# The first FFN's opening stage: fewer, larger contraction groups, and every partial product added by VectorE out of PSUM

## The chip, the cores and the metric

The kernel runs on one core of one Trainium2 chip. The metric is the device time of one execution in microseconds (us). All times below are read from the runs of this kernel or from its profile, which was taken on the chip.

The engines are called by short names: PE (TensorE, the matmuls; PEld is its weight load), DVE (VectorE), ACT (ScalarE), POOL (GpSimd) and SP (SyncE, which here only issues DMAs). SBUF is the on-chip working memory, PSUM the memory into which PE accumulates.

## The reference

One layer of a hybrid encoder on 256 tokens of width 2048, in float32. The part that matters here is the first feed-forward network (FFN) and the modulation in front of it:

```python
mod = (silu(c) @ w_ada + b_ada).reshape(B, 9, D)         # D = 2048
sh1, sc1, ga1, ... = mod
h = rms_norm(x, g_ffn1) * (1.0 + sc1) + sh1
x = x + 0.5 * ga1 * ((silu(h @ w1_a) * (h @ w3_a)) @ w2_a)   # D_FF = 5632
```

Then follow the mixer (latent attention and gated linear attention, merged by gates), a second FFN of the same form, and a last norm. `w_ada` is 2048 x 18432; `w1_a` and `w3_a` are 2048 x 5632.

## The kernel before

**Products.** Every float32 product is computed from exact parts. A weight tile `raw` is split into `wh` (ACT, line 97) and `wl = raw - wh` (DVE, line 98); the activations are kept transposed as `hTh` and `hTl`, 128 rows of the contraction per tile. `mm3` (lines 108 to 111) then issues three matmuls, `wh*hTh`, `wl*hTh` and `wh*hTl`, for each of the two token blocks of 128 tokens.

**Weights.** All weights pass through one ring of three 1 MB buffers, `raws` (line 46), filled by DMAs that SP issues in order. The parts go to `wh` and `wl`, six buffers of 1024 columns each (line 47): one `raw` gives two of each. A unit of `w_ada` goes through the same ring: `ada_unit` (line 159) loads 1 MB and multiplies it by the row `c_bc` on DVE with a running sum (line 163), which gives one column of 128 entries of `mod`.

**The opening stage.** The normed and modulated `h` needs, for each 128 rows of the contraction (`kt`, 16 of them), two columns of `mod` (shift and scale), so two `w_ada` units. The kernel does not wait for all 32. It walks the contraction in groups (`GROUPS`, line 397): as soon as the columns of a group are there, it makes the `h` rows of that group and multiplies them with the matching rows of `w1_a` and `w3_a` for the first six chunks of 512 columns (`NPRO`, line 396). That makes 12 partial products per group (6 chunks, two matrices), each 256 x 512. A partial product goes into a PSUM tile `pacc` (two such tiles, line 49) and is then added to a running sum in SBUF, `sums` (line 494). The loop at lines 458 to 513 emits this raw tile by raw tile; four 128 x 512 weight tiles share one raw buffer, so there are 48 of them.

**How a partial product is added (lines 493 to 508).** The first group's go to `sums` by an ACT copy. Of the later ones, one in three (`ADD_DVE`, line 398) is added by DVE straight from PSUM (line 503). The others are copied by ACT to `ev` (line 507) and added by POOL in SBUF (line 508). In the last group the product of `w1_a` is copied by ACT (line 500) and added by POOL (line 501), then goes through silu on ACT (line 510); that of `w3_a` is added by DVE; POOL multiplies the two (line 512).

**The rows of h.** `xn_T` (line 287) scales the rows of `x` and transposes them on PE; `mod_T` (line 296), here with `early=True`, applies scale and shift on ACT (line 306), casts `hTh` on ACT (line 311) and subtracts to `hTl` on POOL (line 312).

**What sets the order.** `AHEAD` (line 401) says how many raw tiles ahead of a group's first raw tile all of its `w_ada` units must have been issued; between these marks `target` (line 449) spreads the units evenly. `LEAD` and `XLEAD` say how early `mod_T` and `xn_T` are emitted. The program order so written is not yet the order of each engine's queue: a scheduler takes the instructions by program order as their operands become ready by its own estimate, and fixes one order for each engine. On the chip each engine then runs its list in that order.

After the stage come `ffn_down` for the six chunks (line 517), and the remaining five chunks with the plain loop `ffn_up`.

Of the kernel before, what the change touches and what calls it, by code (L numbers as in the profile page):

```python
# [31 lines left out]

# offsets of the columns of `cols`
C_BADA, C_GF1, C_GMX, C_GF2, C_GQL, C_GKV, C_GQN, C_GKN = 0, 144, 160, 176, 192, 196, 200, 201
# offsets of the parts of `rows`
R_GQR, R_GKR, R_GGLA, R_FREQ = 0, 64, 128, 384
# [3 lines left out]
def layer_kernel(ctx: ExitStack, tc: tile.TileContext, a: dict):  # L40
# [17 lines left out]
    def wkA(name):  # L58
        return wk.tile([P, 1024], F32, tag="wA", name=name)
# [3 lines left out]

    # ------------------------------------------------------------ constants
    x_sb = const.tile([P, TB, D], F32, name="x_sb")
# [14 lines left out]

    # ------------------------------------------------------------ weights
    def load_unit(ap, width=2048):
# [4 lines left out]
    def split_raw(raw, src_cols, n):  # L87
        """exact parts of raw[:, :src_cols], as pairs of n columns"""
        res = []
        per = max(1, (src_cols // n) // 2)  # L90
        k = 0
        while k * n < src_cols:
            w = min(per * n, src_cols - k * n)
            wh = hl.tile([P, 1024], F32R, tag="wh", name="wh")
            wl = hl.tile([P, 1024], F32R, tag="wl", name="wl")
            src = raw[:, k * n:k * n + w]
            ACT.copy(wh[:, :w], src)  # L97
            DVE.tensor_tensor(wl[:, :w], src, wh[:, :w].bitcast(F32), op=ALU.subtract)  # L98
            for q in range(w // n):
                res.append((wh[:, q * n:(q + 1) * n], wl[:, q * n:(q + 1) * n]))  # L100
            k += w // n
        return res

    def unit_parts(ap, nkt, n):
        """one weight unit: nkt tiles of n columns"""
        return split_raw(load_unit(ap, nkt * n), nkt * n, n)
# [8 lines left out]
    def gemm(acc, units, n=512, tbm=None, mid=None, hook=None):  # L115
        """acc[tok, n] = x^T W over the units (ap, nkt, k0, xs); units tbm[0]:tbm[1] are
        done for one token block and then for the other"""
        total = sum(u[1] for u in units)
# [35 lines left out]

    # ------------------------------------------------------------ adaLN columns
    ada_q = []
# [14 lines left out]
    def need(j, kt):  # L171
        """issue what is queued up to the unit that gives column kt of mod j"""
        while (j, kt) not in ada_done:
            fill(1)
# [7 lines left out]
    def load_c(pool, first=False):  # L182
        """silu(c) on every partition"""
        c_bc = pool.tile([P, D], F32, tag="cbc", name="c_bc")
        if not first:
            ACT.dma_start(c_bc, a["c"].to_broadcast([P, D]))
            ACT.activation(c_bc, c_bc, AF.Silu)
            return c_bc
        SP.dma_start(c_bc[0:1, :], a["c"])
        ACT.activation(mod[:, 0:16], mhalf, AF.Silu)  # L190
        ps = bank("warm")
        for _ in range(WARM):
            PE.matmul(ps[:, 0:P], ones, ones, start=True, stop=True)
        ACT.activation(c_bc[0:1, :], c_bc[0:1, :], AF.Silu)
        for kg in range(4):
            ps = bank("c_ps")
            PE.matmul(ps, ones[0:1, :], c_bc[0:1, kg * 512:(kg + 1) * 512], start=True, stop=True)
            ACT.copy(c_bc[:, kg * 512:(kg + 1) * 512], ps)
        return c_bc

    def mod_cols(i, lo, hi, c_g):
        """columns lo:hi of (a, b) of norm i"""
        sh, sc = 3 * i * 16, (3 * i + 1) * 16
# [11 lines left out]
    def gate_rows(pool, i, scale, name):  # L215
        """gate i as rows broadcast over the partitions, 512 columns at a time"""
        j = 3 * i + 2
# [23 lines left out]

    # ------------------------------------------------------------ norm into T layout
    ss_t = const.tile([P, TB, 4], F32, name="ss_t")
# [23 lines left out]
    def next_hT(i):  # L267
        """a list that takes h^T of norm i, and what fills it for a token block"""
        hT = []
# [13 lines left out]
    def norm_T(hT, i, tb, k0, nk):  # L283
        """rows k0*128.. of h^T of norm i, in exact parts"""
        mod_T(hT, i, tb, k0, nk, xn_T(tb, k0, nk))
# [10 lines left out]
    def mod_T(hT, i, tb, k0, nk, ps, early=False):  # L296
# [14 lines left out]
        ACT.copy(hi, hv)  # L311
        (POOL if early else DVE).tensor_tensor(lo, hv, hi.bitcast(F32), op=ALU.subtract)  # L312

    # ------------------------------------------------------------ FFN
    def ffn_act(acc1, acc3):
        """silu(acc1) * acc3"""
        s = wkA("silu")
# [6 lines left out]
    def ffn_gT(g, ring, name):  # L324
        """g transposed, in exact parts: [P, 2, 4, S]"""
        gT = ring.tile([P, 2, 4, S], F32R, tag="ring", name=name)
# [12 lines left out]
    def resid(acc, g, n, tbs, tail=False, then=None):  # L339
        """x += acc * gate for the 512 columns n of the token blocks tbs"""  # L340
        nt = len(tbs)
# [12 lines left out]
    def add_product(units, g, n, tail, then, tbm, hook=None):  # L354
        """x += gate * (product) for the 512 columns n"""
        g(n)
# [37 lines left out]

    # ================================================================ FFN 1
    NPRO = 6
    GROUPS = (1, 1) + (2,) * 7
    ADD_DVE = 3
    LEAD = 3
    XLEAD = 1  # L400
    AHEAD = lambda gi: (0, 1, 0, 1, 2, 3, 4, 5, 5)[gi]
    ADA_END = 5
    RATE = 0.75
    LATE = 1
    with tc.tile_pool(name="f1", bufs=1, reuse_waits="tile") as f1, \
# [36 lines left out]
        n_all = len(ada_q)  # L442
        # ada units that have to be issued before a raw tile
        marks = [(0, 2 * GROUPS[0])]
# [13 lines left out]
        for r, grp in enumerate(raws_of):  # L458
# [23 lines left out]
            for gi, c, wi, k in grp:  # L482
# [12 lines left out]
                if gi == 0:  # L495
                    ACT.copy(sums[c][:, wi], acc)
                elif gi == len(GROUPS) - 1 and wi == 0:
                    pre = wkA("silu")
                    pv = pre.rearrange("p (t n) -> p t n", t=TB)
                    ACT.copy(pv, acc)  # L500
                    POOL.tensor_tensor(pv, pv, sums[c][:, 0], op=ALU.add)
                elif (c * 2 + wi) % ADD_DVE == 0 or gi == len(GROUPS) - 1:
                    DVE.tensor_tensor(sums[c][:, wi], acc, sums[c][:, wi], op=ALU.add)  # L503
                else:
                    ev = wkB("ev")
                    evv = ev.rearrange("p (t n) -> p t n", t=TB)
                    ACT.copy(evv, acc)  # L507
                    POOL.tensor_tensor(sums[c][:, wi], sums[c][:, wi], evv, op=ALU.add)  # L508
                if gi == len(GROUPS) - 1 and wi == 1:
                    ACT.activation(pre, pre, AF.Silu)  # L510
                    g = wkB("gact")
                    POOL.tensor_tensor(g, sums[c][:, 1].rearrange("p t n -> p (t n)"), pre, op=ALU.mult)
                    late.append(g)

# [10 lines left out]

    # ================================================================ mixer
    xs = xs_of(hT)
# [15 lines left out]
    with tc.tile_pool(name="mx", bufs=1, reuse_waits="tile") as mx:  # L543
# [4 lines left out]
        with tc.tile_pool(name="mla", bufs=1, reuse_waits="tile") as ml:  # L548
            # ---- rotary tables
            posi = ml.tile([P, TB], I32, name="posi")  # L550
# [66 lines left out]

            # ---- latents
            def latent(parts, c_g, name):
                """RMS-normed latent, transposed, in exact parts; parts: per token block 512 columns"""  # L620
                junk = wkA("junk")
# [36 lines left out]
            kv_done, ckv = latent([acc[:, tb] for tb in range(TB)], C_GKV, "ckv")  # L658
            # query latent, k_rope and g_lr: columns [q 0:256 | k_rope], [q 256:512 | g_lr]
            accs = [acc_tile("qc0"), acc_tile("qc1")]  # L660
# [11 lines left out]

            # ---- k_rope | g_lr
            def rope(dst, src, tab, nh):
                """dst, src [P, TB, nh, 64]"""
                ta, tbb = tab
# [38 lines left out]
            def mla_pair(hp, k_hook):  # L715
                """latents up for two heads; returns the stages of their attention"""
                v4 = lambda t, d: t.rearrange("p (t h d) -> p t h d", t=TB, h=2)
# [135 lines left out]
        with tc.tile_pool(name="late", bufs=1, reuse_waits="tile") as lt, ExitStack() as ctx2:  # L853
# [5 lines left out]
            with tc.tile_pool(name="gla", bufs=1, reuse_waits="tile") as gl:  # L859
# [38 lines left out]
                def gla_head(h, hook):  # L898
                    """one head; returns the stages behind its projections"""
                    hs = slice(h * P, (h + 1) * P)  # L900
# [145 lines left out]

    # ================================================================ FFN 2
    with tc.tile_pool(name="f2", bufs=1, reuse_waits="tile") as f2, \
# [36 lines left out]
def _units(w):  # L1085
    """[K, N] -> [K/512, N/512, 128, 4*512]: 512x512 blocks, rows k*128+p at partition p"""
    K, N = w.shape
# [58 lines left out]
```

## Time and profile before

| | |
|---|---|
| time, median of 3 runs | 2260.61 us (2259.78 to 2260.78) |
| span of the profiled execution, first to last instruction | 2255.0 us |
| time of the median run beyond that span | 5.6 us |
| mean granted TensorE clock | 0.981 |
| first and last start of a matmul into `pacc` | 19.0 and 402.6 us |
| busy in the first 405 us: PE, DVE, ACT, POOL | 326.5, 365.4, 212.2, 233.7 us |

No time of its own is listed for the profiled execution beside its span; the 5.6 us are the difference between the median of the runs and that span. Busy times are sums of the profile's records of an engine; matmuls are pipelined, so a busy PE is not a PE at its peak. Line numbers are those of the kernel before. A row of a group reads: line, engine, operation, output and inputs with their shapes, count, then busy microseconds, the mean nanoseconds of one, and the engine's idle time just before them with what ended it.

### The profile page before, as it was taken

The numbers are of one execution on the slowest core, as the hardware profiler recorded it, in microseconds if no ns is written. First come the engines' busy times: TensorE is split into PE (matmuls) and PEld (weight loads), VectorE is DVE, ScalarE is ACT, GpSimd is POOL, SyncE is SP. The second block draws the span as 40 slices with busy tenths as digits, with TensorE's granted clock in tenths as the row PEclk, the third lists the DMA queues.
The fourth block names the chain that finished last, engine by engine and source line by source line (L and its number), as shares of the span: only waits on it lengthen the run. The fifth ranks groups of instructions, "written<-read, shape, count | busy, mean of one in ns | idle before, by whom it ended". The sixth has DMA issues, their size and how long they took to land.

```text
span 2255.0 us, 24933 instructions
## 1 busy us (share of the span) xinstructions
PE 2161.3 (96%) x9652; PEld 1763.1 (78%) x9652; DVE 1578.9 (70%) x1604; ACT 1044.3 (46%) x1279; POOL 276.6 (12%) x148
## 2 busy tenths in 40 slices
PE   8788788999999999999999999999999999999998
PEld 5566566788888887988777788878888888888886
DVE  6999898888787787756566667766666455444454
ACT  6545455433433445555564444455444433444443
POOL 1766557100000000001000000000000000000000
PEclk8899899999999999999999999999999999999999
DMA  8667675799898884644576777866777555555553
GB/s 297 230 233 253 227 248 192 276 352 347 334 336 324 328 318 148 227 145 165 195 256 245 257 262 278 296 235 241 281 287 268 191 208 196 189 193 187 194 189 112
DMA packets 87305, 549.16 MB, mean 244 GB/s; under 512 B 10322, under 2 KB 10626, under 8 KB 28435
## 3 DMA queue, kind: packets, MB, share of 16 engines
q1 hardware_dynamic: 84242, 539.97, 66.4%
q0 software_dynamic: 1344, 3.17, 0.5%
q10 hardware_dynamic: 1602, 4.44, 0.5%
q8 instruction: 75, 1.23, 0.2%
q14 instruction: 42, 0.34, 0.0%
HBM read 545.42 MB, written 2.12 MB: 243 GB/s over the span
## 4 chain that ended last, share of the span: by engine, by line
PE 82%; DVE 7%; issue 4%; DMA 3%; POOL 2%; ACT 1%; SPq 0%; POOLq 0%; DVEq 0%; ACTq 0%
PE a L109 10%; PE a L111 10%; PE a L110 10%; PE y L111 8%; PE y L110 8%; PE y L109 8%; DVE wl L98 3%; DMA raw<-in_w_a 2%; DVE raw L163 2%; POOL sum L508 1%; PE qkv L109 1%; PE ga L109 1%; PE gb L109 1%; PE ga L111 1%; PE qkv L111 1%
## 5 line engine op out<-in xcount | busy, mean ns | idle before, releaser
L98 DVE TENSOR_TENSOR wl<-raw,wh 128x1024 fp32r<-128x1024 f32 (+1 forms) x744 | 959.3, 1305 | 522.8 <-ACT wh L97 520.7
L97 ACT CAST wh<-raw 128x1024 fp32r<-128x1024 f32 (+1 forms) x744 | 765.5, 1042 | 965.2 <-PE a L111 283.7
L109 PE MATMUL a<-wh,hTh 128*128 128x512 f32 x1024 | 399.8, 390 | 0.3 <-ACT hTh L311 0.3
L111 PE MATMUL a<-wh,hTl 128*128 128x512 f32 x1024 | 399.0, 390 | 0.0
L110 PE MATMUL a<-wl,hTh 128*128 128x512 f32 x1024 | 398.6, 389 | 0.0
L163 DVE SCALAR_TENSOR_TENSOR raw<-raw,c_bc 128x2048 f32<-128x2048 f32 x144 | 351.1, 2438 | 38.1 <-DMA raw<-in_w_ada 37.7
L109 PE MATMUL y<-wh,gT 128*128 128x512 f32 x704 | 275.1, 391 | 0.0
L111 PE MATMUL y<-wh,gT 128*128 128x512 f32 x704 | 274.2, 389 | 0.0
L110 PE MATMUL y<-wl,gT 128*128 128x512 f32 x704 | 274.2, 389 | 0.0
L111 PEld LDWEIGHTS a<-wh,hTl 128*128 128x128 f32 x1024 | 192.2, 188 | 41.0 <-DVE hTl L312 0.8
L109 PEld LDWEIGHTS a<-wh,hTh 128*128 128x128 f32 x1024 | 192.3, 188 | 39.9 <-ACT hTh L311 0.6
L110 PEld LDWEIGHTS a<-wl,hTh 128*128 128x128 f32 x1024 | 192.3, 188 | 39.3
L109 PE MATMUL pacc<-wh,hTh 128*128 128x512 f32 x384 | 166.7, 434 | 56.0 <-DVE sum L503 50.1
L508 POOL TENSOR_TENSOR sum<-sum,ev 128x1024 f32<-128x1024 f32 x56 | 172.6, 3093 | 121.2 <-ACT ev L507 121.1
L110 PE MATMUL pacc<-wl,hTh 128*128 128x512 f32 x384 | 163.0, 424 | 11.3 <-DVE wl L98 11.3
L111 PE MATMUL pacc<-wh,hTl 128*128 128x512 f32 x384 | 161.0, 419 | 1.7 <-POOL hTl L312 1.7
L109 PEld LDWEIGHTS y<-wh,gT 128*128 128x128 f32 x704 | 132.2, 188 | 28.1
L111 PEld LDWEIGHTS y<-wh,gT 128*128 128x128 f32 x704 | 132.2, 188 | 27.3
L110 PEld LDWEIGHTS y<-wl,gT 128*128 128x128 f32 x704 | 132.2, 188 | 27.2
L109 PEld LDWEIGHTS pacc<-wh,hTh 128*128 128x128 f32 x384 | 79.4, 207 | 86.2 <-DVE sum L503 53.4
L507 ACT COPY ev<-pacc 128x1024 f32<-128x1024 f32 x56 | 56.8, 1014 | 106.1 <-PE pacc L111 100.6
L110 PEld LDWEIGHTS pacc<-wl,hTh 128*128 128x128 f32 x384 | 79.7, 207 | 29.9 <-DVE wl L98 13.8
(296 smaller groups left out, 2487.6 us busy)
## 6 DMA issues: line engine op xcount, KB each, us to landing
raw<-in_w_ada SPq DMA_DIRECT2D x144, 1024.0 KB, 5.2
raw<-in_w_b SPq DMA_DIRECT2D x132, 1024.0 KB, 4.8
raw<-in_w_a SPq DMA_DIRECT2D x84, 1024.0 KB, 5.8
raw<-in_w_in SPq DMA_DIRECT2D x60, 1024.0 KB, 4.8
raw<-in_w_a SPq DMA_DIRECT2D x84, 512.0 KB, 5.0
raw<-in_w_out SPq DMA_DIRECT2D x16, 1024.0 KB, 5.6
raw<-in_w_proj_a SPq DMA_DIRECT2D x8, 1024.0 KB, 4.9
raw<-in_w_proj_b SPq DMA_DIRECT2D x8, 1024.0 KB, 4.8
```

The costliest lines, as they stand in the source:

```text
L97: ACT.copy(wh[:, :w], src)
L98: DVE.tensor_tensor(wl[:, :w], src, wh[:, :w].bitcast(F32), op=ALU.subtract)
L109: PE.matmul(out, xh, wh, start=start, stop=False)
L110: PE.matmul(out, xh, wl, start=False, stop=False)
L111: PE.matmul(out, xl, wh, start=False, stop=stop)
L163: DVE.scalar_tensor_tensor(out=raw, in0=raw, scalar=1.0, in1=c_bc, op0=ALU.mult, op1=ALU.mult, accum_out=dst)
L507: ACT.copy(evv, acc)
L508: POOL.tensor_tensor(sums[c][:, wi], sums[c][:, wi], evv, op=ALU.add)
```

## The change

`GROUPS` becomes 1, 1, 2, 4, 4, 4 (six groups instead of nine), and `AHEAD` gets a value for each of the six. Every partial product after the first group is added by DVE out of PSUM. In the last group silu reads the running sum after that add, and the product of the two halves is made by DVE. The subtraction that gives `hTl` is made by DVE in the early rows too. POOL keeps no addition, subtraction or product of this stage. The rest of the diff removes comments and docstrings.

```diff
@@ mod_T
         ACT.copy(hi, hv)
-        (POOL if early else DVE).tensor_tensor(lo, hv, hi.bitcast(F32), op=ALU.subtract)
+        DVE.tensor_tensor(lo, hv, hi.bitcast(F32), op=ALU.subtract)
...
@@ FFN 1
     NPRO = 6
-    GROUPS = (1, 1) + (2,) * 7
-    ADD_DVE = 3
+    GROUPS = (1, 1, 2, 4, 4, 4)
     LEAD = 3
     XLEAD = 1
-    AHEAD = lambda gi: (0, 1, 0, 1, 2, 3, 4, 5, 5)[gi]
+    AHEAD = lambda gi: (0, 1, 1, 2, 4, 5)[gi]
...
                 if gi == 0:
                     ACT.copy(sums[c][:, wi], acc)
-                elif gi == len(GROUPS) - 1 and wi == 0:
-                    pre = wkA("silu")
-                    pv = pre.rearrange("p (t n) -> p t n", t=TB)
-                    ACT.copy(pv, acc)
-                    POOL.tensor_tensor(pv, pv, sums[c][:, 0], op=ALU.add)
-                elif (c * 2 + wi) % ADD_DVE == 0 or gi == len(GROUPS) - 1:
-                    DVE.tensor_tensor(sums[c][:, wi], acc, sums[c][:, wi], op=ALU.add)
-                else:
-                    ev = wkB("ev")
-                    evv = ev.rearrange("p (t n) -> p t n", t=TB)
-                    ACT.copy(evv, acc)
-                    POOL.tensor_tensor(sums[c][:, wi], sums[c][:, wi], evv, op=ALU.add)
-                if gi == len(GROUPS) - 1 and wi == 1:
-                    ACT.activation(pre, pre, AF.Silu)
-                    g = wkB("gact")
-                    POOL.tensor_tensor(g, sums[c][:, 1].rearrange("p t n -> p (t n)"), pre, op=ALU.mult)
-                    late.append(g)
+                    continue
+                DVE.tensor_tensor(sums[c][:, wi], acc, sums[c][:, wi], op=ALU.add)
+                if gi == len(GROUPS) - 1:
+                    if wi == 0:
+                        pre = wkA("silu")
+                        ACT.activation(pre, sums[c][:, 0].rearrange("p t n -> p (t n)"), AF.Silu)
+                    else:
+                        g = wkB("gact")
+                        DVE.tensor_tensor(g, sums[c][:, 1].rearrange("p t n -> p (t n)"), pre, op=ALU.mult)
+                        late.append(g)
```

## The prediction

> **What bounds the kernel now.** I read the page's slices first, then the busy time by windows, then DVE's groups inside and outside the stage, the queues of DVE and POOL side by side, and last who waited for whom.
>
> ```profile
> span 2255.0 us, 24933 instructions
> DVE  6999898888787787756566667766666455444454
> POOL 1766557100000000001000000000000000000000
> ```
>
> A slice is 56 us. POOL works only in the first seven, and DVE is at its busiest there. Those slices are the opening stage. The windows, with columns length, then busy us and records for each engine, granted PE clock, DMA share, GB/s:
>
> ```profile
> core 0: us, PE busy (x) PEld busy (x) DVE busy (x) ACT busy (x) POOL busy (x), PEclk, DMA share, GB/s
> 0.00:60.00 60.00, 47.98 (x172) 34.17 (x172) 42.04 (x55) 39.27 (x54) 13.45 (x16) 0.86 0.85 292
> 60.00:82.00 22.00, 13.21 (x38) 9.28 (x39) 22.00 (x14) 10.58 (x16) 19.52 (x7) 0.77 0.52 175
> 82.00:405.00 323.00, 265.32 (x1061) 208.40 (x1060) 301.40 (x200) 162.38 (x197) 200.69 (x71) 0.92 0.68 234
> 416.00:600.00 184.00, 184.00 (x815) 151.96 (x814) 147.51 (x135) 70.52 (x74) 3.26 (x6) 1.00 0.91 345
> ```
>
> From 82 to 405 us DVE is busy 301.4 of 323 us, 93%. DMA moves 234 GB/s there against 345 right after the stage, and ACT is half idle, so neither is the bound. After the stage PE issues 815 matmuls in 184 us, 0.226 us each. That is PE's pace when nothing holds it. The stage's own matmuls and adds, as first and last start:
>
> ```profile
> L109 PE MATMUL pacc<-wh,hTh x384: 387/389/797, 19.0 to 401.7; 128*128 128x512 f32 x192
> L111 PE MATMUL pacc<-wh,hTl x384: 387/389/797, 20.1 to 402.6; 128*128 128x512 f32 x192
> L507 ACT COPY ev<-pacc x56: 1005/1015/1023, 46.7 to 351.3; 128x1024 f32<-128x1024 f32 x56
> L503 DVE TENSOR_TENSOR sum<-pacc,sum x34: 1209/1211/1225, 46.1 to 405.6; 128x1024 f32<-128x1024 f32 x34
> ```
>
> The three matmul lines have 384 each, 1152 in all; at 0.226 us they need 260 us. They take 402.6 - 19.0 = 383.6. So PE loses some 123 us in this stage, and the question is how much of that DVE gives back.
>
> How full PE is here depends on the record. By matmuls it is 265.3 of 323 us, which leaves 58 us; by weight loads it is 208.4 of 323 (65%) against 152.0 of 184 (83%) in the stretch where PE never waits, so the same loads would fit in 252 us and 71 us are free. The Trainium skill (Perfetto Trace Analysis, Identifying the Most-Contended Engine) says that matmul busy time is a poor measure of how near TensorE is to its limit and that weight-load busy time is a good one; by it the window can give 71 us, by matmul busy time 58. The 0.226 us pace bears the page out.
>
> **Why DVE is slow in the stage.** Its groups in the first 405 us, then from 416 to 600 us where POOL does nothing with tiles:
>
> ```profile
> L98 DVE TENSOR_TENSOR wl<-raw,wh 128x1024 fp32r<-128x1024 f32 x100 | 188.9, 1916 | 23.2 <-ACT wh L97 23.1
> L163 DVE SCALAR_TENSOR_TENSOR raw<-raw,c_bc 128x2048 f32<-128x2048 f32 x38 | 108.7, 2861 | 5.9 <-DMA raw<-in_w_ada 5.8
> L503 DVE TENSOR_TENSOR sum<-pacc,sum 128x1024 f32<-128x1024 f32 x33 | 40.0, 1213 | 4.4 <-PE pacc L111 4.4
> L208 DVE TENSOR_TENSOR ab<-mod,small 128x2 f32<-128x2 f32 (+1 forms) x9 | 10.7, 1189 | 0.1
> L212 DVE SCALAR_TENSOR_TENSOR ab<-modt,small 128x2 f32<-128x2 f32 (+1 forms) x9 | 7.9, 879 | 0.3
> L210 DVE TENSOR_TENSOR modt<-mod,small 128x2 f32<-128x2 f32 (+1 forms) x9 | 5.7, 631 | 0.2
> ```
>
> ```profile
> L98 DVE TENSOR_TENSOR wl<-raw,wh 128x1024 fp32r<-128x1024 f32 x69 | 81.7, 1221 | 32.6 <-ACT wh L97 32.3
> L163 DVE SCALAR_TENSOR_TENSOR raw<-raw,c_bc 128x2048 f32<-128x2048 f32 x25 | 57.1, 2285 | 3.6 <-DMA raw<-in_w_ada 3.6
> L163 DVE DVE_READ_ACCUMULATOR raw<-raw,c_bc 128x1 f32 x24 | 2.0, 82 | 0.0
> L336 DVE TENSOR_TENSOR gT<-gT_ps,gT 128x512 fp32r<-128x512 f32 x2 | 1.3, 682 | 0.0
> L321 DVE TENSOR_TENSOR gact<-a,silu 128x1024 f32<-128x1024 f32 x1 | 1.2, 1224 | 0.0
> L227 DVE TENSOR_TENSOR gcol<-mod,small 128x4 f32<-128x4 f32 x3 | 0.5, 159 | 0.1
> ```
>
> The same subtraction takes 1.916 us in the stage and 1.184 us of DVE time after it (81.7/69; neighbours overlap a little). A `mod` unit takes 2.861 against 2.284, an addition of two columns up to 1.189 against 0.159. The add out of PSUM, with one operand in SBUF, keeps its 1.21 us. The two queues side by side, start and length, say who is in the way:
>
> ```profile
> 197.88 5.08 DVE L98 TENSOR_TENSOR wl<-raw,wh 128x1024 fp32r<-128x1024 f32 x2
> 207.26 1.21 DVE L503 TENSOR_TENSOR sum<-pacc,sum 128x1024 f32<-128x1024 f32 x1
> ```
>
> ```profile
> 198.51 6.67 POOL L508 TENSOR_TENSOR sum<-sum,ev 128x1024 f32<-128x1024 f32 x2
> 205.95 3.59 POOL L508 TENSOR_TENSOR sum<-sum,ev 128x1024 f32<-128x1024 f32 x1 [0.77 <-ACT ev L507]
> ```
>
> Two subtractions from SBUF take 5.08 us under two POOL adds; the PSUM add inside POOL's third takes its normal time. So DVE's instructions with two SBUF operands lose time to POOL's, and the PSUM add does not.
>
> **The change, part by part.**
>
> *POOL leaves the stage.* Its two main groups there:
>
> ```profile
> L508 POOL TENSOR_TENSOR sum<-sum,ev 128x1024 f32<-128x1024 f32 x56 | 172.6, 3093 | 121.2 <-ACT ev L507 121.1
> L312 POOL TENSOR_TENSOR hTl<-hf,hTh 128x256 fp32r<-128x256 f32 (+1 forms) x18 | 24.7, 1383 | 24.5 <-ACT hTh L311 24.5
> ```
>
> At the later stretch's durations DVE gets back 188.9 - 100 x 1.184 = 70.5 us on the subtractions, 108.7 - 38 x 2.284 = 21.9 on the `mod` units, and 24.3 - 27 x 0.16 = 20.0 on the three small lines: 112.4 us.
>
> *More adds on DVE.* Five groups of 12 are 60 adds against 34, so 26 more at 1.21: +31.5 us. All of it is on the engine that sets the pace. Nine groups with all adds on DVE would have been 96; the larger groups are what holds it to 60.
>
> *The product of the halves*, six at 1.224 (the same operation with one PSUM operand is the nearest row; bounds 1.18 and 1.31, the subtraction's two means): +7.3 us.
>
> *hTl on DVE*: six of 128x512, two of 128x256, four of 128x128. The first at 0.682 (the 128x512 subtraction), the smaller between 0.16 and 0.682, taken as 0.3: +5.9 us (bounds 5 to 8).
>
> *ACT loses 56 + 6 copies* of about 1.015 us. ACT is not the bound, but its queue was: a copy `ev` that waits for PE holds the next `wh` cast behind it, and DVE's `wl` waits for that cast. The waits of the first 420 us (total, times, longest):
>
> ```profile
> ACT ev L507 <- PE pacc L111: 100.6, 40, 8.1
> PEld pacc L109 <- DVE sum L503: 53.4, 20, 5.4
> DVE wl L98 <- ACT wh L97: 26.5, 15, 4.1
> PEld pacc L110 <- DVE wl L98: 13.8, 8, 4.4
> DVE sum L503 <- PE pacc L111: 4.4, 3, 1.9
> ```
>
> I count no gain for it beyond DVE's present idle time, because the wait for PE moves to DVE's queue: what stands behind a waiting add there is the next `mod` unit and the next two `wl`, and PE waits for those.
>
> *DMAs.* The 48 raw tiles and 37 `mod` units stay; a raw tile of a group of four is one 1 MB transfer instead of two halves, on the same SP queue. The `mod` units come earlier: by the tenth raw tile 16 are issued instead of 11 (from the marks that `AHEAD` sets). At 345 GB/s the 85 MB need some 246 us, covered by DVE's work; uncovered they are a floor below both others. POOL's later DMAs for the gate rows no longer stand behind its products; they were not waited for.
>
> *The sum for DVE.* Busy in 0 to 405: 42.0 + 22.0 + 301.4 = 365.4; 39.6 idle, of which 18.0 in the first 60 us, where the first data are awaited. After: 365.4 - 112.4 + 31.5 + 7.3 + 5.9 = 297.7. The 18.0 stay. The later idle time is 21.6 now; with PE's 260 us so near, DVE will wait for PE somewhat more often, so I take 25, between 0 and 65 (below). 297.7 + 18 + 25 = 341 against 405: 64 us less. Behind the stage PE is busy all of 184 us, so the gain passes through whole. Made on the span it is 2255.0 - 64 = 2191; with the 5.6 us by which the median run exceeds that span, 2197.
>
> **The rivals.**
>
> *Accumulators freed late (2240).* Only DVE frees `pacc` now, and there are two. Today 34 adds cause 20 waits of PE, 2.67 us each. If 60 adds cause them at the same rate, they are 94 us; shortened as the subtractions in front of them are (1.184/1.916 = 0.62), 58. Add the waits for `wl`, 13.8 x 0.62 = 9, some 10 of smaller ones, and the low clock's loss: of the 123 us about 92 are waits, so some 31 are clock, 26 for fewer waits. 19 + 260 + 58 + 9 + 10 + 26 = 382, 21 us gained. For: the wait is today's longest on PE. Against: an accumulator of four tiles lasts PE 24 x 0.226 = 5.4 us instead of 2.7, so the other one has twice the time to be freed.
>
> *Nearly full overlap (2172).* DVE never waits after the first 60 us, since ACT's casts run ahead: 298 + 18 = 316, 89 us gained. For: DVE waited only 4.4 us for PE. Against: PE's floor is 19 + 260 = 279, and two engines so near each other seldom mesh.
>
> *Lockstep, slower (2309).* If DVE's order is the program's, the add of raw tile r stands ahead of `wl` of r+1, and PE idles over it. Per tile of a group of four: 5.4 + 1.21 (add) + 21/36 x 2.37 (`mod` units) + 1.18 (`wl`) = 9.2 us; 36 tiles are 331. The first 12 tiles take 24 x 1.184 + 16 x 2.37 + 24 x 1.21 = 95, and with 18 idle and some 7 of small work 120. 451 against 402.6 is 48 slower. It decides from 7.85 us a tile, two thirds of that chain exposed. Against: the 4.4 us wait in three times says that DVE's queue runs behind PE's, not ahead.
>
> *POOL was not the cause (2305).* Then DVE keeps its long instructions and only gains work: 365.4 + 44.7 + 39.6 = 450, 45 us slower. Against it stand the rows above: the same subtraction is short as soon as POOL rests, though DMA is then at its busiest. The Trainium skill (Perfetto Trace Analysis, Optimizing Scalar/DVE Operations) advises moving work from a saturated VectorE to ScalarE or GpSimd, which speaks against this change; but it warns that between GpSimd and VectorE this may not help, because they share an SBUF read port. By the advice alone the time would be this rival's 2305, by the warning the forecast's; the 1.916 against 1.184 us side with the warning.
>
> **How the numbers follow.** Forecast 0.57 (its own range 2175 to 2220, later idle time 3 to 48 us), accumulators freed late 0.20, nearly full overlap 0.11, lockstep 0.06, POOL not the cause 0.03, and 0.03 for gains eaten elsewhere with no net change. The predicted time is 2197. From 2168, just under full overlap, to 2243, just over the late accumulators, the range leaves out the slower cases, no change, and part of the tails. A measurement of this kernel can tell about 0.2% from no change, 4.5 us. Faster 0.88, same 0.03, slower 0.09.
>
> **What would show it.** POOL's row of the slices near zero; `wl` at 1.2 us and `mod` units at 2.3 in the stage; 60 adds at 1.21; the last matmul into `pacc` near 338 us; DVE about 298 us busy until then; granted clock above 0.92. The forecast is wrong if `wl` stays near 1.9 us, if PE's wait for `sum` passes 80 us, or if DVE's wait for `pacc` grows to tens of us.

## The result, and the profile after

The changed kernel takes 2182.4 us (median of 4 runs, 2181.6 to 2185.7) against 2260.2 before on the same chip: 78 us less, a ratio of 0.9654 with a 95% interval of 0.9640 to 0.9667. The forecast was 2197. The ratios here compare executions at the usual granted clock; one of the kernel before (3584 us, clock 0.555) and one of a variant (2507 us, clock 0.798) stand apart from the rest and are left out of them. The profiled span fell from 2255.0 to 2180.4 us, by 74.6. The last matmul into `pacc` starts at 327.9 instead of 402.6 us, 74.7 earlier. So the whole gain of the profiled execution lies in the opening stage, and nothing of it was lost behind it.

The page's slices of the changed kernel:

```profile
span 2180.4 us, 24712 instructions
DVE  7999997877887868555666677766765555444554
POOL 0000000000000001000000000000000000000000
PEclk8899999999999999999999999999999999999999
```

POOL is empty in the stage. The busy time by windows (length, busy us and records of each engine, granted PE clock, DMA share, GB/s):

```profile
core 0: us, PE busy (x) PEld busy (x) DVE busy (x) ACT busy (x) POOL busy (x), PEclk, DMA share, GB/s
0.00:60.00 60.00, 47.97 (x178) 33.77 (x178) 45.04 (x65) 35.88 (x49) 1.87 (x8) 0.89 0.84 295
60.00:82.00 22.00, 15.11 (x56) 11.63 (x57) 21.79 (x25) 7.64 (x12) 0.00 (x0) 0.84 0.77 260
82.00:330.00 248.00, 238.21 (x1036) 192.91 (x1037) 226.97 (x215) 109.83 (x132) 0.00 (x0) 0.98 0.80 295
```

From 82 us on, DVE is still busy 92% of the time, as before. But PE is now at 96% with a clock of 0.98, instead of 82% at 0.92. DVE's groups in the first 330 us:

```profile
L98 DVE TENSOR_TENSOR wl<-raw,wh 128x1024 fp32r<-128x1024 f32 x102 | 122.1, 1220 | 13.9 <-ACT wh L97 13.3
L163 DVE SCALAR_TENSOR_TENSOR raw<-raw,c_bc 128x2048 f32<-128x2048 f32 x37 | 84.5, 2284 | 3.7 <-DMA raw<-in_w_ada 2.4 <-ACT c_bc L198 1.3
L497 DVE TENSOR_TENSOR sum<-pacc,sum 128x1024 f32<-128x1024 f32 x60 | 72.7, 1219 | 11.3 <-PE pacc L111 11.0
L504 DVE TENSOR_TENSOR gact<-sum,silu 128x1024 f32<-128x1024 f32 x5 | 6.1, 1216 | 0.0
L312 DVE TENSOR_TENSOR hTl<-hf,hTh 128x512 fp32r<-128x512 f32 (+2 forms) x12 | 5.8, 507 | 1.4 <-ACT hTh L311 1.4
L208 DVE TENSOR_TENSOR ab<-mod,small 128x4 f32<-128x4 f32 (+2 forms) x6 | 0.9, 156 | 0.1
```

The subtraction (1.220 us), the `mod` unit (2.284) and the small addition (0.156) have the durations that the stretch behind the stage showed before the change (1.221, 2.285 and 0.159). The waits of the first 345 us answer to those shown of before (total, times, longest):

```profile
PEld pacc L109 <- ACT wh L97: 14.8, 9, 2.9
DVE wl L98 <- ACT wh L97: 14.8, 17, 2.3
PEld pacc L110 <- DVE wl L98: 12.7, 14, 3.2
DVE sum L497 <- PE pacc L111: 11.0, 16, 2.0
PEld pacc L109 <- DVE sum L497: 2.3, 2, 1.9
```

PE's wait for its accumulators, 53.4 us in 20 times before, is 2.3 us in two. Instead DVE's adds now wait for PE a little, 11.0 us in 16 times. (PE's waits in this list are those of its weight load, PEld; a wait of PE itself for the same cause can stand beside it in the profile and is not to be added to it.)

Where in the stage the gain lies is seen by counting the matmuls into `pacc` in two windows, first before the change, then after:

```profile
0.00:120.00 120.00, 79.93 (x290) 59.41 (x291) 9.71 (x8) 27.14 (x28) 0.87 0.75 258
120.00:405.00 285.00, 225.87 (x864) 174.69 (x862) 30.32 (x25) 47.66 (x47) 0.91 0.67 231
```

```profile
0.00:120.00 120.00, 78.97 (x277) 56.85 (x277) 26.29 (x22) 11.91 (x12) 0.87 0.82 285
120.00:330.00 210.00, 202.10 (x876) 163.43 (x875) 46.39 (x38) 0.00 (x0) 1.00 0.80 296
```

(Columns: PE, PEld, DVE, ACT, then clock and DMA.) In the first 120 us the changed kernel does 277 matmuls, 13 fewer than before. All of the gain comes after that: the remaining 875 take 207.9 us, the 862 of before took 282.6. At PE's pace of 0.226 us a matmul, PE's lost time is the window less the matmuls' need, counted from the first matmul near 19 us:

| | matmuls by 120 us | PE lost by 120 us | PE lost later | last matmul into `pacc` |
|---|---|---|---|---|
| before | 290 | 36 | 88 | 402.6 |
| changed | 277 | 38 | 10 | 327.9 |

"Lost" here is what is left over, so it holds waits, PE's other work and matmuls that take longer than 0.226 us. After 120 us, PE stood idle for 52.7 us before the change and 3.6 after it, some 49 of the 78 us. Most of the rest lies in the matmuls: 864 records took 225.4 us at a granted clock of 0.91, 876 took 201.7 at 1.00, that is 0.261 and 0.230 us each (the ends of matmuls are modelled, so this division is an estimate). Whether the clock rose because PE waited less, no run shows.

### The profile page after: what moved, and what is told of

Its sections match the earlier page's. It is cut to its first block, busy times and chain, and to the rows that moved or that the text cites. A ratio compares the mean times of both kernels' runs of the same rounds, so it can differ in the third digit from the quotient of the medians.

```text
span 2180.4 us, 24712 instructions
## 1 busy us (share of the span) xinstructions
PE 2136.3 (98%) x9652; PEld 1750.1 (80%) x9652; DVE 1506.2 (69%) x1639; ACT 984.5 (45%) x1205; POOL 42.4 (2%) x62
## 4 chain that ended last, share of the span: by engine, by line
PE 91%; DVE 4%; DMA 2%; issue 2%; ACT 1%; POOL 0%; SPq 0%; POOLq 0%; DVEq 0%; ACTq 0%
PE a L109 11%; PE a L111 11%; PE a L110 11%; PE y L109 8%; PE y L110 8%; PE y L111 8%; PE pacc L110 3%; PE pacc L111 3%; PE pacc L109 3%; DMA raw<-in_w_a 2%; PE qkv L109 1%; PE ga L109 1%; PE gb L109 1%; PE ga L111 1%; PE qkv L111 1%
## 5 line engine op out<-in xcount | busy, mean ns | idle before, releaser
L98 DVE TENSOR_TENSOR wl<-raw,wh 128x1024 fp32r<-128x1024 f32 (+1 forms) x744 | 889.1, 1209 | 519.8 <-ACT wh L97 517.3
L163 DVE SCALAR_TENSOR_TENSOR raw<-raw,c_bc 128x2048 f32<-128x2048 f32 x144 | 329.1, 2286 | 32.2 <-DMA raw<-in_w_ada 30.3
L109 PE MATMUL pacc<-wh,hTh 128*128 128x512 f32 x384 | 155.7, 406 | 14.6 <-ACT wh L97 9.5
L110 PE MATMUL pacc<-wl,hTh 128*128 128x512 f32 x384 | 155.3, 404 | 8.4 <-DVE wl L98 8.2
L111 PE MATMUL pacc<-wh,hTl 128*128 128x512 f32 x384 | 152.9, 398 | 0.0
L109 PEld LDWEIGHTS pacc<-wh,hTh 128*128 128x128 f32 x384 | 73.9, 192 | 37.4 <-ACT wh L97 14.8
L110 PEld LDWEIGHTS pacc<-wl,hTh 128*128 128x128 f32 x384 | 74.4, 194 | 27.6 <-DVE wl L98 12.7
L111 PEld LDWEIGHTS pacc<-wh,hTl 128*128 128x128 f32 x384 | 74.5, 194 | 15.5
L497 DVE TENSOR_TENSOR sum<-pacc,sum 128x1024 f32<-128x1024 f32 x60 | 72.7, 1219 | 11.3 <-PE pacc L111 11.0
```

The source lines that it names most:

```text
L109: PE.matmul(out, xh, wh, start=start, stop=False)
L110: PE.matmul(out, xh, wl, start=False, stop=False)
L111: PE.matmul(out, xl, wh, start=False, stop=stop)
L163: DVE.scalar_tensor_tensor(out=raw, in0=raw, scalar=1.0, in1=c_bc, op0=ALU.mult, op1=ALU.mult, accum_out=dst)
```

## The experiments

The theory under test was the prediction's: POOL's instructions that read SBUF stretch DVE's, DVE sets the pace, and the change gives DVE 112 us back at a price of 45. The rivals were the regrouping by itself, ACT's queue, and a bound that is no longer DVE's. The comparisons are with the kernel before on the same chip, and the same table of lost time is extended at the end.

### The two halves of the change, each alone

The new groups with the old division of the adds (short diff against the kernel before):

```diff
-    GROUPS = (1, 1) + (2,) * 7
+    GROUPS = (1, 1, 2, 4, 4, 4)
-    AHEAD = lambda gi: (0, 1, 0, 1, 2, 3, 4, 5, 5)[gi]
+    AHEAD = lambda gi: (0, 1, 1, 2, 4, 5)[gi]
```

> The kernel before with the new groups (1, 1, 2, 4, 4, 4) and their AHEAD, the adds divided between DVE and POOL as before: 22 adds on DVE, 32 + 6 + 6 additions and products and the 12 subtractions of hTl on POOL. Theory (DVE sets the stage's pace, POOL's work with SBUF operands stretches DVE's): POOL has 56 instructions instead of 86, so about two thirds of the 112 us of stretching stay, some 73; DVE busy about 365 - 39 - 12 x 1.21 = 312, stage end near 350 us, time 2200 to 2220. Rival (the gain is the regrouping: fewer and later evictions, POOL does not matter): nearly all of the gain, 2180 to 2190, with wl near its mean of before, 1.9 us. If the regrouping gives nothing: 2255 or more.

Measured: 2215.3 us, ratio 0.9806 (0.9779 to 0.9832), 44 us gained. The last matmul into `pacc` starts at 356.7 us, and DVE is busy 303.4 of 365 us. DVE and POOL in the first 365 us:

```profile
L98 DVE TENSOR_TENSOR wl<-raw,wh 128x1024 fp32r<-128x1024 f32 x101 | 159.9, 1614 | 38.3 <-ACT wh L97 38.3
L503 DVE TENSOR_TENSOR sum<-pacc,sum 128x1024 f32<-128x1024 f32 x22 | 26.7, 1216 | 3.7 <-PE pacc L111 3.7
```

```profile
L508 POOL TENSOR_TENSOR sum<-sum,ev 128x1024 f32<-128x1024 f32 x32 | 93.0, 2912 | 140.6 <-ACT ev L507 140.5
```

With 56 instructions on POOL instead of 86, the subtraction takes 1.614 us: between 1.916 and 1.220. The regrouping does not stand for nearly all of the gain. With less work on POOL the stretching is smaller too, so part of what the regrouping gives may come by way of POOL; the run does not separate the two.

The other half, all adds on DVE with the old groups (against the changed kernel):

```diff
-    GROUPS = (1, 1, 2, 4, 4, 4)
+    GROUPS = (1, 1) + (2,) * 7
-    AHEAD = lambda gi: (0, 1, 1, 2, 4, 5)[gi]
+    AHEAD = lambda gi: (0, 1, 0, 1, 2, 3, 4, 5, 5)[gi]
```

> The changed kernel with the old groups 1, 1, 2 x 7 and their AHEAD: 96 adds, all on DVE, nothing on POOL. Theory: wl 1.22 us and mod units 2.28 as in the changed kernel, DVE busy 294 + 36 x 1.21 = 338, with 36 idle the stage ends near 374 us, time 2220 to 2232. Rival (the gain is the regrouping): 2250 to 2265. Rival (accumulators are freed late once DVE alone frees them): PE waits for sum as much as before, 50 us or more, time 2240 or more.

Measured: 2218.5 us, ratio 0.9817 (0.9790 to 0.9844), 41 us gained, just better than the theory's range. DVE in the first 350 us:

```profile
L98 DVE TENSOR_TENSOR wl<-raw,wh 128x1024 fp32r<-128x1024 f32 x98 | 117.3, 1218 | 4.7 <-ACT wh L97 4.7
L497 DVE TENSOR_TENSOR sum<-pacc,sum 128x1024 f32<-128x1024 f32 x96 | 116.3, 1220 | 5.5 <-PE pacc L111 5.3
```

DVE is busy 326.1 of 350 us, 12 less than expected, and PE's wait for `sum` is 12.6 us in 24 times. So 36 more adds on DVE cost less than taking POOL out gains. The stage ends at 348.3 us, 54 us earlier than before. Of these 13 us are lost behind it: in the profiled execution the span after that point is 1865.4 us, against 1852.4 before (1859.0 with the groups alone). From 405 us on PE waits 6.6 us for parts of `w2_a`, which it does not in the kernels before and after; where the rest goes was not followed.

The two halves give 44 and 41 us, together 78; the times alone cannot tell this from a plain sum, since each half is known to some 6 us. The ends of the stage can: they come 46 and 54 us earlier, and with both halves 75, not 100. That fits halves which take in part from the same DVE time, and a whole that runs into another limit (below).

### POOL kept busy, reading SBUF and only writing it

```diff
                 DVE.tensor_tensor(sums[c][:, wi], acc, sums[c][:, wi], op=ALU.add)
+                POOL.tensor_tensor(dmy, x_sb[:, :, 0:384], sums[c][:, wi, :, 0:384], op=ALU.add)
+                POOL.tensor_tensor(dmy, x_sb[:, :, 0:384], sums[c][:, wi, :, 0:384], op=ALU.add)
```

> The changed kernel with two additions on POOL behind each of the 60 adds; they read x_sb and the running sum in SBUF (128x768) into a tile that nobody reads. DVE's own work is the same. Theory: POOL is busy some 216 us in the stage, about as before, wl goes back to 1.6 to 1.9 us and DVE gains 70 to 110 us, stage end 400 to 440, time 2250 to 2290. Rival (DVE was slow for its dependencies or for PSUM, not for POOL): wl stays at 1.22 us, time 2180 to 2190.

Measured: 2307.2 us, ratio 1.0215 (1.0198 to 1.0231), slower than the kernel before. The last matmul into `pacc` starts at 442.8 us. DVE and POOL in the first 455 us:

```profile
L98 DVE TENSOR_TENSOR wl<-raw,wh 128x1024 fp32r<-128x1024 f32 x102 | 207.4, 2058 | 7.6 <-ACT wh L97 7.6
L163 DVE SCALAR_TENSOR_TENSOR raw<-raw,c_bc 128x2048 f32<-128x2048 f32 x37 | 121.7, 3288 | 2.9 <-DMA raw<-in_w_ada 1.5 <-ACT c_bc L198 1.3
L498 DVE TENSOR_TENSOR sum<-pacc,sum 128x1024 f32<-128x1024 f32 x60 | 72.2, 1212 | 1.9 <-PE pacc L111 1.9
```

```profile
L499 POOL TENSOR_TENSOR dmy<-x_sb,sum 128x768 f32<-128x768 f32 x60 | 165.1, 2752 | 104.7 <-DVE sum L498 98.5 <-DVE modt L210 3.4
```

POOL's work, of no use to anybody, brings the stretching back and more: 85 us on the subtractions and 37 on the `mod` units. The time is 17 us above the expected range, since DVE is busy 435.5 us and not the 404 at most that I had reckoned with. The add out of PSUM stays at 1.21 us. So POOL is the cause of the stretching, not a dependency or PSUM. The run also shows that DVE sets the pace when it is loaded so: DVE is busy 435.5 of 455 us, the subtractions and `mod` units take 122 us longer than in the changed kernel, and the last matmul into `pacc` starts 115 us later.

The same with work that hardly reads:

```diff
+                POOL.tensor_tensor(dmy[:, 0, 0:1], x_sb[:, 0, 0:1], sums[c][:, wi, 0, 0:1], op=ALU.add)
+                POOL.memset(dmy, 0.0)
+                POOL.memset(dmy, 0.0)
+                POOL.memset(dmy, 0.0)
```

> The changed kernel with three memsets of 128x768 on POOL behind each of the 60 adds, each three led by an addition of one column that ties them to the add. POOL is busy but hardly reads SBUF. If only what POOL reads from SBUF stands in DVE's way (so the Trainium skill, SBUF - State Buffer, Who interferes with whom): wl stays near 1.22 us, time 2180 to 2190. If any work of POOL in SBUF does: wl stretches with POOL's busy time, 40 to 80 us more, 2220 to 2265.

Measured: 2182.1 us, ratio 0.9661 (0.9646 to 0.9677), that of the changed kernel. DVE and POOL in the first 345 us:

```profile
L98 DVE TENSOR_TENSOR wl<-raw,wh 128x1024 fp32r<-128x1024 f32 x105 | 125.6, 1220 | 16.7 <-ACT wh L97 16.2
```

```profile
L499 POOL TENSOR_TENSOR dmy<-x_sb,sum 128x1 f32<-128x1 f32 x60 | 61.2, 1021 | 117.7 <-DVE sum L498 110.6 <-DVE modt L210 5.2
L500 POOL MEMSET dmy<- 128x768 f32 x60 | 44.5, 742 | 3.6
```

POOL is busy 192 of the first 330 us, the same share as before the change (233.7 of 405), and DVE does not notice. The Trainium skill (SBUF — State Buffer, Who interferes with whom) says that a VectorE instruction with two SBUF inputs contends with a GpSimd instruction that reads SBUF and not with one that only writes it; these two runs agree with it, 2.058 against 1.220 us for the same subtraction.

### ACT's copies back in ACT's queue

```diff
-                DVE.tensor_tensor(sums[c][:, wi], acc, sums[c][:, wi], op=ALU.add)
+                ev = wkB("ev")
+                evv = ev.rearrange("p (t n) -> p t n", t=TB)
+                ACT.copy(evv, acc)
+                DVE.tensor_tensor(sums[c][:, wi], evv, sums[c][:, wi], op=ALU.add)
```

> The changed kernel, but each of the 60 products is first copied out of PSUM by ACT (as before the change) and then added by DVE in SBUF; nothing on POOL. DVE's work is the same (1.18 to 1.22 us an add). Theory (DVE's load and POOL's contention made the difference, ACT's copies did not): the same time within some 8 us, 2175 to 2192. Rival (the gain came from taking the copies that wait for PE out of ACT's queue, where they held up the wh casts): ACT waits for pacc by tens of us again, wl waits for wh more than 25 us, time 2200 to 2225.

Measured: 2184.2 us, ratio 0.9664 (0.9648 to 0.9681). The copies do wait for PE again,

```profile
ACT ev L499 <- PE pacc L111: 73.9, 44, 6.8
```

73.9 us, and DVE's adds wait for the copies 14.8 us in 20 times. But DVE's wait for `wh` stays at 11.5 us, where the rival asked for more than 25, and the stage ends at 327.6 us. The adds with both operands in SBUF:

```profile
L500 DVE TENSOR_TENSOR sum<-ev,sum 128x1024 f32<-128x1024 f32 x60 | 72.7, 1221 | 14.9 <-ACT ev L499 14.8
```

They take 1.221 us, as long as those out of PSUM (1.219). So in the changed kernel freeing ACT's queue gave nothing that can be measured, and with POOL at rest reading PSUM directly does not make the adds cheaper. What the copies cost ACT's queue in the kernel before, where POOL worked too, no run takes apart.

### Only hTl back on POOL

```diff
-        DVE.tensor_tensor(lo, hv, hi.bitcast(F32), op=ALU.subtract)
+        (POOL if early else DVE).tensor_tensor(lo, hv, hi.bitcast(F32), op=ALU.subtract)
```

> The changed kernel with only the 12 subtractions of hTl back on POOL. DVE has 5.8 us less, POOL reads SBUF for some 10 to 17 us. Theory: its neighbours on DVE are stretched by about what POOL works, so DVE gains nothing or loses up to 10 us, time 2180 to 2192. If POOL's work is free: 2174 to 2179.

Measured: 2185.2 us, ratio 0.9667 (0.9651 to 0.9683): no difference that can be told from the changed kernel (2182.4 and, on another chip, 2185.1). DVE and POOL in the first 330 us:

```profile
L98 DVE TENSOR_TENSOR wl<-raw,wh 128x1024 fp32r<-128x1024 f32 x100 | 121.1, 1233 | 19.1 <-ACT wh L97 18.6
L163 DVE SCALAR_TENSOR_TENSOR raw<-raw,c_bc 128x2048 f32<-128x2048 f32 x37 | 86.3, 2331 | 8.0 <-DMA raw<-in_w_ada 8.0
```

```profile
L312 POOL TENSOR_TENSOR hTl<-hf,hTh 128x512 fp32r<-128x512 f32 (+2 forms) x12 | 13.4, 1124 | 217.6 <-ACT hTh L311 217.6
```

The subtraction takes 1.233 us instead of 1.220 and the `mod` unit 2.331 instead of 2.284. So 13.4 us of POOL stretch these neighbours by some 3 us, about half of the 5.8 us that DVE is spared and less than the theory had. The time would not show it either way, as the next run explains.

### Is DVE still the bound?

```diff
+        w = 1024 if j < 2 else 2048
-        DVE.scalar_tensor_tensor(out=raw, in0=raw, scalar=1.0, in1=c_bc, op0=ALU.mult,
-                                 op1=ALU.mult, accum_out=dst)
+        DVE.scalar_tensor_tensor(out=raw[:, :w], in0=raw[:, :w], scalar=1.0, in1=c_bc[:, :w],
+                                 op0=ALU.mult, op1=ALU.mult, accum_out=dst)
```

> The changed kernel, in which DVE multiplies and sums only the first 1024 of the 2048 columns of the 32 w_ada units of the first norm; so half of each sum behind shift and scale is left out. The transfers are the same, DVE has 32 x 1.1 = 35 us less. If DVE still sets the stage's pace after the change: last matmul into pacc at 293 to 305 us, time 2147 to 2162. If PE, the arrival of weights or the ring of three buffers does: 318 to 328 us, time 2172 to 2182.

Measured: 2182.1 us, ratio 0.9656 (0.9637 to 0.9675). Nothing is gained. The two windows of all engines, and their sum:

```profile
0.00:120.00 120.00, 94.84 (x356) 69.57 (x357) 86.00 (x123) 56.21 (x80) 1.56 (x8) 0.87 0.82 292
120.00:330.00 210.00, 206.27 (x923) 169.01 (x922) 177.75 (x182) 97.42 (x115) 0.70 (x1) 1.00 0.79 296
sum 330.00, PE 301.11 PEld 238.58 DVE 263.75 ACT 153.63 POOL 2.26; mean PE 150.55 PEld 119.29 DVE 131.88 ACT 76.82 POOL 1.13
```

DVE is 30 us lighter, 263.8 instead of 293.8, and the stage ends at 326.2 instead of 327.9. After the change DVE no longer sets the pace. From 120 us on PE does, busy 206 of 210 us at a granted clock of 1.00. Before 120 us PE loses 37 us here too, with DVE busy only 86 of 120 us instead of 100.7, so DVE's load is not what holds it. The next run takes the transfers as well:

```diff
-        raw = load_unit(a["w_ada"][j, kt])
+        w = 1024 if j < 2 else 2048
+        raw = load_unit(a["w_ada"][j, kt][:, :w], w)
```

(with the same half sum on DVE)

> The changed kernel, in which the 32 w_ada units of the first norm load only the first 1024 of their 2048 columns and DVE sums only those; so half of each sum behind shift and scale is left out, and 16 of the stage's 87 MB are not moved. DVE's work is that of the run with half sums alone, which gained nothing. If the arrival of the units holds PE in the first 120 us: 8 MB less before the twelfth raw tile at 285 GB/s is up to 28 us, last matmul into pacc at 300 to 314 us, time 2155 to 2170. If the order of the work or the latency of each transfer does: 322 to 329 us, time 2175 to 2184.

Measured: 2172.5 us, ratio 0.9618 (0.9599 to 0.9638), 13 us less than the changed kernel on the same chip (2185.1), the stage ends at 319.8 us. That is between the two ranges for the time and for the last matmul. The matmuls into `pacc` in the first 120 us:

```profile
0.00:120.00 120.00, 86.28 (x324) 63.15 (x325) 30.22 (x25) 11.98 (x12) 0.91 0.72 239
```

324 instead of 277. So the transfers of the units are part of what holds PE early, some 9 of the 38 us. The rest is hardly bytes: DMA moves only 239 GB/s here, against 285 in the changed kernel. What it is, this run does not say. The trace of the changed kernel shows at least who waits: PE, ACT and the DMA queue (SPq) in the first 120 us, ACT's from 19 us on.

```profile
PE pacc L109 <- ACT wh L97: 9.5, 5, 2.5
PE pacc L110 <- DVE wl L98: 5.0, 4, 2.9
ACT wh L97 <- DMA raw<-in_w_a: 36.4, 13, 8.0
SPq L84 <- DVE raw L163: 28.9, 9, 6.8
SPq L476 <- DVE wl L98: 21.2, 7, 7.2
```

Of the 38 us PE stands idle for 19; some 16 are matmuls that take longer than 0.226 us, at a granted clock of 0.89 between 19 and 120 us. PE waits for the parts of the weights, ACT for the weights to land, and the DMA queue for DVE to free one of the three `raw` buffers. That points to the round trip of this ring, but no run changed the number of its buffers, so this stays open.

### Other groups

The early loss belongs to the first groups, so two other divisions were tried, both with 48 adds instead of 60.

```diff
-    GROUPS = (1, 1, 2, 4, 4, 4)
+    GROUPS = (1, 3, 4, 4, 4)
-    AHEAD = lambda gi: (0, 1, 1, 2, 4, 5)[gi]
+    AHEAD = lambda gi: (0, 1, 2, 4, 5)[gi]
```

> The changed kernel with groups 1, 3, 4, 4, 4 and AHEAD 0, 1, 2, 4, 5: 48 adds instead of 60, so DVE has 12 x 1.22 = 14.6 us less, but PE has to wait for six w_ada units behind the first group instead of two. If DVE's sum of work decides: last matmul into pacc near 314 us, time 2166 to 2172. If the early wait for PE's next rows decides: no gain, 2180 to 2195, with a gap on PE of 15 to 25 us before 60 us.

Measured: 2173.4 us, ratio 0.9609 (0.9589 to 0.9628). The last matmul into `pacc` starts at 314.4 us, where the theory that DVE's sum decides had it, and the time is 1.4 us above its range. Yet the run with half sums shows that DVE's sum doesn't decide, so the number is met by chance. The run was repeated beside the changed kernel on one chip:

> Groups 1, 3, 4, 4, 4 once more, now on the same chip beside the changed kernel. If the first measurement holds: 2167 to 2177 us and 6 to 14 us under the changed kernel. If it was the chip: within 4 us of it.

> The changed kernel once more as the measure for the other three of these runs: 2178 to 2186 us.

Measured: 2171.0 us, ratio 0.9610 (0.9595 to 0.9625), and 2185.1 us for the changed kernel, 0.9670 (0.9655 to 0.9684). In this second profile of the changed kernel the stage ends at 331.0 us instead of 327.9, so differences of 3 us between single profiles mean nothing. The groups 1, 3, 4, 4, 4 beat both kernels, the changed one by 14 us. Their matmuls into `pacc` in the two windows of the second run:

```profile
0.00:120.00 120.00, 85.80 (x326) 64.43 (x327) 15.84 (x13) 12.20 (x12) 0.90 0.89 324
120.00:330.00 210.00, 190.48 (x828) 154.33 (x826) 42.79 (x36) 0.00 (x0) 1.00 0.79 289
```

The gain is early: 326 matmuls by 120 us instead of 277, with DMA at 324 GB/s instead of 285. The expected gap on PE of 15 to 25 us before 60 us did not show: by then 107 matmuls are done instead of 122, 3 us of PE's pace, and the lead is won between 60 and 120 us. It is not won by fewer `mod` units, of which DVE sums 19 by 120 us instead of 17.

The second division:

```diff
-    GROUPS = (1, 1, 2, 4, 4, 4)
+    GROUPS = (2, 2, 4, 4, 4)
-    AHEAD = lambda gi: (0, 1, 1, 2, 4, 5)[gi]
+    AHEAD = lambda gi: (0, 1, 2, 4, 5)[gi]
```

> The changed kernel with groups 2, 2, 4, 4, 4 and AHEAD 0, 1, 2, 4, 5: 48 adds, no group of one row and so no raw tile of four small transfers; PE starts later, near 28 us. By PE's pace (260 us behind the start, 16 lost later, some 10 early): last matmul into pacc near 314 us, time 2165 to 2175. If the later start isn't made up: 320 us or more, 2176 to 2190.

Measured: 2173.9 us, ratio 0.9624 (0.9605 to 0.9643). PE starts 5.4 us later, at 24.3, and makes it up: 313 matmuls by 120 us, the stage ends at 319.2. The time lies in the expected range, the end of the stage 5 us behind the expected 314.

PE's lost time once more, in us, by the same working as in the first table:

| | matmuls by 120 us | PE lost by 120 us | PE lost later | DVE busy, us in window | median us |
|---|---|---|---|---|---|
| before | 290 | 36 | 88 | 365.4 in 405 | 2260.2 |
| groups alone | 240 | 47 | 31 | 303.4 in 365 | 2215.3 |
| adds on DVE alone | 324 | 27 | 41 | 326.1 in 350 | 2218.5 |
| changed | 277 | 38 | 10 | 293.8 in 330 | 2182.4 |
| half sums | 284 | 37 | 10 | 263.8 in 330 | 2182.1 |
| half loads | 324 | 29 | 13 | 268.5 in 330 | 2172.5 |
| 1, 3, 4, 4, 4 (second run) | 326 | 27 | 9 | 290.6 in 330 | 2171.0 |

The regrouping of the change costs PE 11 us early, whether POOL works (36 to 47) or not (27 to 38), and saves later.

## Why the prediction came out as it did

**Right in direction and size, 15 us too slow.** The gain was 78 us where 64 were forecast; the time lies in the stated range and inside the forecast's own (2175 to 2220). Of the difference some 11 us lie in the sum for the stage (330 instead of 341). The other 3.6 lie in the step from the span to the median run: the forecast took over 5.6 us from before, and it is 2.0 after. The prediction's words that POOL works only in the first seven slices leave out a rest in the eighth and one slice later on, which changes nothing.

**POOL's leaving: right.** 112.4 us were to come back. The changed kernel's `wl` takes 1.220 us, its `mod` units 2.284, its small additions 0.156. The run with idle work on POOL shows that it is POOL, and the run with memsets that POOL's writing to SBUF does not do it. That leaves what an add does beyond a memset, reading SBUF first of all; a POOL instruction that computes without reading SBUF was not run.

**The added work: right.** 60 adds at 1.219, the products at 1.216 and `hTl` at 5.8 us in all were put at 1.21, 1.224 and 5.9.

**DVE's sum: 298 forecast, 294 measured,** within 330 us. The 18 us of early idle time are 15, the 25 later are 21. These terms add up to the end of the stage whatever sets its pace, so that they fit does not show that DVE does.

**That DVE would still set the pace: wrong.** The sum "DVE's work plus its idle time" came near the end of the stage because DVE and PE are so close, not because DVE decides; that the number came out within 15 us is in this part luck. Before the change DVE did set the pace: of PE's waits after 120 us, 40.2 us were for `sum` and 10.2 for `wl`. Taking 30 us of DVE's work away moves the stage by 1.7 us. What stands in its place is PE's own account: 19 us to the first matmul, 260 of matmuls, 38 lost in the first 120 us and 10 after, together the 328 at which the stage ends. What is lost is measured here and follows from no rule. The forecast's 341 priced the later waits by DVE's idle time. PE's floor stood in the text, 279, and was used only as a bound.

**No gain before 120 us: not seen.** The forecast spread the relief over the whole stage. The first third gained nothing; the adds on DVE alone, with the old groups, do 324 matmuls by then. The new groups ask for more `mod` units early, 17 summed by 120 us instead of 13, which the prediction reckoned in MB and put under DVE's work. But that is not the whole cause: half the bytes give back 9 us, and the groups 1, 3, 4, 4, 4 sum 19 units by 120 us and still do 326 matmuls. What the first three groups cost PE stays open.

**The rivals.** *Accumulators freed late* fell: PE's wait for `sum` is 2.3 us, not 58. The argument against it, twice the time per accumulator, explains at most a small part: with the old groups, where an accumulator has no more time than before, 96 adds on DVE cause waits of only 12.6 us. *Nearly full overlap* (2172) came closer than its chance of 0.11: DVE's idle time is 15 + 21 instead of 18, but PE loses hardly anything after 120 us. *Lockstep* fell: DVE waits 11.0 us for PE in 16 times. *POOL was not the cause* fell. ACT's queue was counted at nothing, and the run with the copies back agrees: 2184 us.

**The two records of PE.** By weight loads 71 us were free between 82 and 405 us, by matmuls 58. The stage became 75 us shorter, more than either, and nearer to the weight loads; so the rule of the Trainium skill (Perfetto Trace Analysis, Identifying the Most-Contended Engine) was the better guide here. The pace of 0.226 us, which the prediction named beside it, would have left 323 - 1061 x 0.226 = 83 us free. I had used neither in the sum.

## What to carry to other kernels

When an engine looks saturated, compare one of its instructions with the same instruction in a stretch where its neighbour rests: 1.92 against 1.22 us, over all such instructions, said that a third of DVE's time (112 of 365 us) was POOL's doing, and that giving POOL work cost DVE more than doing it. Before adding up the relieved engine's new total, take the next engine's floor and its losses and see which is later; after a relief of this size the pace can change hands, as it did here, and a run that takes a further piece of work away tells it at once. A change that gains late may lose early: split the stage and count matmuls in each part.

## What the runs showed of the hardware

POOL's adds in SBUF hold up DVE's instructions with two SBUF operands; POOL's memsets don't. With 192 us of POOL in the stage, some 130 of them memsets of 0.742 us, the subtraction takes 1.220 us. With two adds per product, 335.7 us busy in 455, it takes 2.058. Small DVE instructions are held as well as large ones: an addition of two columns took up to 1.189 us before the change, against 0.159 for one of four columns with POOL at rest. What the contention costs POOL no run shows, since none has the same POOL instruction with DVE at rest. A DVE add with one operand in PSUM is not held: 1.213 before, 1.219 after, 1.212 under POOL's idle work.
